# Row maxima that skip NaN: VectorE's write-backs end with tile 33, and the tiles behind it are divided anew into loads, passes and maxima

## The chip, the core and the metric

The kernel runs on one core of a Trainium2 chip. The metric is the time of one execution in microseconds (us) on the device; lower is better. The engines that matter are VectorE (DVE in the profile), ScalarE (ACT), GpSimd (POOL), and SyncE (SP), whose queue issues every load. TensorE does nothing here.

## The reference

```python
x = np.random.randn(32, 2048, 2048).astype(np.float32)
x[np.random.rand(32, 2048, 2048) < 0.1] = np.nan
def reference(x, axis):          # axis = -1
    return np.nanmax(x, axis=axis).astype(np.float32)
```

65536 rows of 2048 float32 numbers, a tenth of them NaN, are reduced to the largest number of each row that is not NaN. 537 MB are read and 0.26 MB written.

## The kernel before

The rows are spread over 128 partitions, so that each partition has 512 rows, 2048 quarters of a row (a quarter, Q, is 512 numbers). They are worked through in 69 tiles: tile 0 has 4 quarters, tiles 1 to 35 have 32, tiles 36 to 68 have 28. Three buffers `xt` take the tiles in turn, so tile n is loaded into the buffer of tile n-3.

A tile goes through four steps.

- SyncE issues its loads, one or several, as soon as the last maximum of tile n-3 is done (line 494).
- ScalarE makes passes (line 298, operation `Prelu`): from the upper 16 bits of each number it makes a key of 16 bits in which a NaN has become harmless. Up to tile 37 the key takes the place of the upper half in `xt`; from tile 38 on the keys stand in one of three key buffers (the names `kt` and, for the two that lie in the room between the buffers, `xt`).
- A write-back turns keys into upper halves again (times -1, plus a constant). GpSimd, ScalarE or VectorE can do it (lines 308, 298 and 315 `TENSOR_SCALAR`).
- VectorE takes the maxima (line 315 `TENSOR_REDUCE`), which need the write-backs of all their quarters.

At the end GpSimd and VectorE put NaN into rows that held nothing else (lines 330, 344, 322), and three stores write the result.

The order on every engine is the order in which the program records the work; nothing is moved afterwards, and semaphores hold an instruction back until what it reads is there. What is recorded is set by the table `TILES`, written out by hand, with one entry for each tile: the sizes of its loads; its passes, in groups, with the write-backs that follow each group; and the sizes of its maxima, all in quarters.

```python
    + [([32], [([12], [(5, -1), 7]), ([12], [12]), ([8], [8])], [12, 12, 8])] * 31
```

This is one load of 32 quarters, a pass of 12 followed by write-backs of 5 and 7, a pass of 12 with one of 12, a pass of 8 with one of 8, and maxima of 12, 12 and 8. A bare number is GpSimd's write-back. A pair names another engine:

```python
who = "pool" if wait is None else "act" if wait == 0 else "dve"
```

so `(5, -1)` is a write-back of 5 quarters by VectorE, `(7, 0)` one of 7 by ScalarE at once, and `(2, 1)` one of 2 by ScalarE after its next pass. The buffer's release and the load that waits for it are these lines:

```python
if state["red"] == len(reds):
    free[number % BUFS] = [state["end"]]
...
xt, before = room(number), free[number % BUFS]
```

Of the kernel before, what the change touches and what calls it, by code (L numbers as in the profile page):

```python
# [15 lines left out]

TILES = (
    [([4], [([4], [4])], [4])]
    + [([32], [([12], [(5, -1), 7]), ([12], [12]), ([8], [8])], [12, 12, 8])] * 31
# [8 lines left out]
    + [([28], [([7], [7]), ([9], [9]), ([12], [12])], [16, 12])] * 2  # L28
# [27 lines left out]
)  # L56


# [582 lines left out]
```

## Time and profile before

| | us |
|---|---|
| median of 3 runs (lowest to highest) | 1266.52 (1262.43 to 1266.83) |
| the profiled execution's own time | 1266.14 |
| its span, first to last instruction | 1264.0 |
| VectorE busy | 1194.2 |
| ScalarE busy | 1125.6 |
| GpSimd busy | 1073.0 |

The span is what the profile's times count in; the execution takes about 2 us more around it. In the views, `a <- b: us, times, longest` is idle time of a that ended when b was done; a row of the order of time has its start, its length, the engine, the line, the operation, what it writes and reads, and in brackets the idle time before it.

### The profile page before, as it was taken

How to read it: one execution, taken by the hardware profiler on the slowest of the kernel's cores; microseconds unless marked ns; L12 is line 12 of the kernel's file. 1: busy time of each engine (PE TensorE's matmuls, PEld its weight loads, DVE VectorE, ACT ScalarE, POOL GpSimd, SP SyncE). 2: the span in 40 equal slices, each digit the busy share in tenths (PEclk: the TensorE clock that was granted, in tenths of full speed). 3: DMA queues.
4: the chain of work that ended last, by engine and by line, in shares of the span. 5: the costliest groups of instructions: out<-in, count | busy, mean ns of one | idle time of the engine just before them, and what ended most of it. 6: DMA issues, size and time to landing. Idle time of an engine off the chain costs nothing.

```text
span 1264.0 us, 1010 instructions
## 1 busy us (share of the span) xinstructions
DVE 1194.2 (94%) x251; ACT 1125.6 (89%) x275; POOL 1073.0 (85%) x248
## 2 busy tenths in 40 slices
DVE  0899999999999999999999999998989989999999
ACT  3999999999999999999999877689777788989998
POOL 0888788888888888888899897867999989999998
DMA  9999999999999999999999999899999999999997
GB/s 413 442 440 431 431 431 431 431 432 431 431 431 438 444 440 433 436 431 431 422 436 433 376 385 436 377 436 436 434 430 414 436 436 426 435 428 433 429 428 307
DMA packets 16807, 537.20 MB, mean 425 GB/s; under 512 B 2592, under 2 KB 2592, under 8 KB 5152
## 3 DMA queue, kind: packets, MB, share of 16 engines
q1 hardware_dynamic: 16800, 537.14, 98.9%
q14 instruction: 7, 0.06, 0.0%
HBM read 536.87 MB, written 0.26 MB: 425 GB/s over the span
## 4 chain that ended last, share of the span: by engine, by line
DVE 38%; DMA 30%; ACT 17%; POOL 14%; issue 1%; SPq 0%; DVEq 0%; ACTq 0%
DVE acc L315 36%; DMA xt<-in_x_dram 30%; ACT xt L298 16%; POOL xt L308 14%; DVE xt L315 2%; ACT kt L298 1%; POOL late L330 0%; POOL acc L344 0%; SPq L285 0%; DVE acc L322 0%; DVEq L182 0%; SPq L636 0%; ACTq L182 0%; SPq L292 0%
## 5 line engine op out<-in xcount | busy, mean ns | idle before, releaser
L315 DVE TENSOR_REDUCE acc<-xt 128x3 f32<-128x6144 f32 (+3 forms) x210 | 1113.4, 5349 | 48.6 <-POOL xt L308 44.4
L308 POOL TENSOR_SCALAR xt<-xt 128x3584 int16<-128x3584 uint16 (+11 forms) x198 | 922.1, 4657 | 180.2 <-ACT xt L298 171.8
L298 ACT ACTIVATE xt<-xt 128x6144 uint16<-128x6144 int16 (+10 forms) x214 | 948.2, 4526 | 117.8 <-DMA xt<-in_x_dram 117.1
L298 ACT ACTIVATE kt<-xt 128x6144 uint16<-128x6144 int16 (+11 forms) x43 | 142.0, 3322 | 13.9 <-POOL xt L308 11.8
L308 POOL TENSOR_SCALAR xt<-kt 128x2048 int16<-128x2048 uint16 (+9 forms) x35 | 143.7, 4107 | 4.8 <-ACT kt L298 2.8
L315 DVE TENSOR_SCALAR xt<-xt 128x2560 int16<-128x2560 uint16 (+3 forms) x38 | 75.9, 1997 | 19.0 <-ACT xt L298 19.0
L298 ACT ACTIVATE xt<-kt 128x1536 int16<-128x1536 uint16 (+4 forms) x16 | 36.9, 2309 | 0.4
L315 DVE TENSOR_SCALAR xt<-kt 128x4096 int16<-128x4096 uint16 x2 | 8.0, 4020 | 0.0
L330 POOL TENSOR_SCALAR late<-acc 128x112 int32<-128x112 f32 (+1 forms) x5 | 4.9, 971 | 0.4
L298 ACT ACT_TABLE_LOAD x1 | 1.3, 1283 | 1.4 <-SPq L292 1.4
L344 POOL TENSOR_TENSOR acc<-acc,late 128x112 int32<-128x112 int32 (+1 forms) x5 | 2.0, 400 | 0.4
L350 POOL MEMSET scalars<- 128x1 f32 x1 | 0.1, 99 | 1.0 <-SPq L292 1.0
L622 POOL MEMSET const-float32-0.0<- 128x1 f32 x1 | 0.1, 99 | 0.2 <-issue 0.2
L298 ACT ACTIVATE scalars<-scalars 128x1 f32<-128x1 f32 x1 | 0.2, 203 | 0.0
L322 DVE SCALAR_TENSOR_TENSOR acc<-acc 128x7 f32<-128x7 f32 x1 | 0.2, 166 | 0.0
L622 POOL MEMSET const-bfloat16-1.0<- 128x1 bf16 x1 | 0.1, 103 | 0.0
L622 POOL MEMSET const-uint8-127<- 128x1 uint8 x1 | 0.1, 103 | 0.0
L622 POOL MEMSET const-float32-1.0<- 128x1 f32 x1 | 0.1, 99 | 0.0
## 6 DMA issues: line engine op xcount, KB each, us to landing
xt<-in_x_dram SPq DMA_DIRECT2D x21, 7168.0 KB, 22.4
xt<-in_x_dram SPq DMA_DIRECT2D x2, 4864.0 KB, 18.4
xt<-in_x_dram SPq DMA_DIRECT2D x4, 2304.0 KB, 26.8
xt<-in_x_dram SPq DMA_DIRECT2D x2, 4352.0 KB, 22.3
xt<-in_x_dram SPq DMA_DIRECT2D x2, 3584.0 KB, 25.4
xt<-in_x_dram SPq DMA_DIRECT2D x5, 1280.0 KB, 27.8
xt<-in_x_dram SPq DMA_DIRECT2D x2, 3072.0 KB, 20.6
xt<-in_x_dram SPq DMA_DIRECT2D x3, 2048.0 KB, 25.2
```

The costliest lines, as they stand in the source:

```text
L298: lambda: nc.scalar.activation(**kw),
L308: lambda: nc.gpsimd.tensor_scalar(**kw),
L315: return order.add("dve", nc.vector, lambda: do(**kw), deps)
L322: lambda: engine.scalar_tensor_tensor(out=acc, in0=acc, scalar=0.0, in1=acc, op0=ALU.mult, op1=ALU.add),
L330: lambda: engine.tensor_scalar(out=none, in0=acc, scalar1=LEAST, scalar2=float(0x00400000), op0=ALU.is_lt, op1=ALU.mult,),
L344: lambda: engine.tensor_tensor(out=bits, in0=bits, in1=none, op=ALU.add),
L350: e_top = order.add("pool", nc.gpsimd, lambda: nc.gpsimd.memset(top, EDGE), [])
L622: nc = _bacc.Bacc("TRN2", target_bir_lowering=False, num_devices=1)
```

## The change

Only the table `TILES` changes. Tile 32 becomes like tiles 1 to 31. Tile 33 keeps a write-back of 5 quarters by VectorE, and that is the last one; tiles 34, 35, 36, 37, 39, 42 and 46 had one each, of 2, 2, 4, 5, 4, 8 and 8 quarters. Tiles 33 to 68 get other loads, passes, write-backs and maxima; their sizes in total (32 and 28 quarters) and their buffers stay. There are 110 loads instead of 111 and 211 maxima instead of 210.

```diff
-    + [([32], [([12], [(5, -1), 7]), ([12], [12]), ([8], [8])], [12, 12, 8])] * 31
-    + [([23, 9], [([18, 6], [(6, -1), 6, 12]), ([8], [8])], [12, 12, 8])]
-    + [([19, 13], [([12], [(5, -1), 7]), ([10], [10]), ([10], [3, 7])], [12, 12, 8])]
-    + [([12, 20], [([12], [(2, -1), 10]), ([12], [12]), ([8], [8])], [12, 12, 8])]
-    + [([15, 17], [([12, 8, 6, 6], [(2, -1), 10, 5, 7, 8])], [12, 12, 8])]
-    + [([28], [([9], [5, (4, -1)]), ([7], [7]), ([7], [7]), ([5], [5])], [4, 12, 12])]
-    + [([28], [([10], [(5, -1), 5]), ([6], [6]), ([9], [9]), ([3], [3])], [16, 12])]
...
+    + [([32], [([12], [(5, -1), 7]), ([12], [12]), ([8], [8])], [12, 12, 8])] * 32
+    + [([18, 14], [([12], [(5, -1), 7]), ([6], [6]), ([6], [6]), ([8], [8])], [12, 12, 8])]
+    + [([12, 20], [([7, 8, 9, 8], [7, 8, 9, 8])], [12, 12, 8])]
+    + [([25, 7], [([6], [6]), ([6], [6]), ([7], [7]), ([5], [(2, 1), 3]), ([8], [8])], [12, 12, 8])]
+    + [([28], [([7], [7]), ([8], [8]), ([9], [9]), ([4], [4])], [4, 8, 3, 1, 4, 8])]
+    + [([28], [([11, 11], [10, 7, 5]), ([6], [6])], [8, 8, 4, 8])]
...
```

What stands in VectorE's row from tile 33 to the first maxima of tile 36 before (`TENSOR_SCALAR` is a write-back, `128x2560` its 5 quarters; `TENSOR_REDUCE` is a maximum, `128x3` its 3 rows):

```order
L315 TENSOR_SCALAR xt<-xt 128x2560
L315 TENSOR_REDUCE acc<-xt 128x3 x2
L315 TENSOR_REDUCE acc<-xt 128x2
L315 TENSOR_SCALAR xt<-xt 128x1024
L315 TENSOR_REDUCE acc<-xt 128x3 x2
L315 TENSOR_REDUCE acc<-xt 128x2
L315 TENSOR_SCALAR xt<-xt 128x1024
L315 TENSOR_REDUCE acc<-xt 128x3 x2
L315 TENSOR_REDUCE acc<-xt 128x2
L315 TENSOR_SCALAR xt<-xt 128x2048
L315 TENSOR_REDUCE acc<-xt 128x1
```

And the same place now (all lines behind the table have numbers smaller by 4):

```order
L311 TENSOR_SCALAR xt<-xt 128x2560
L311 TENSOR_REDUCE acc<-xt 128x3 x2
L311 TENSOR_REDUCE acc<-xt 128x2
L311 TENSOR_REDUCE acc<-xt 128x3 x2
L311 TENSOR_REDUCE acc<-xt 128x2
L311 TENSOR_REDUCE acc<-xt 128x3 x2
L311 TENSOR_REDUCE acc<-xt 128x2
L311 TENSOR_REDUCE acc<-xt 128x1
L311 TENSOR_REDUCE acc<-xt 128x2
L311 TENSOR_REDUCE xt<-xt 128x1
```

The write-backs ahead of the maxima of tiles 34, 35 and 36 are gone; the maxima of 34 and 35 are cut as before, those of 36 into six, one of which leaves its result in `xt` for the next.

GpSimd's row from tile 33 to tile 35 before, each row a write-back:

```order
L308 TENSOR_SCALAR xt<-xt 128x3584
L308 TENSOR_SCALAR xt<-xt 128x5120
L308 TENSOR_SCALAR xt<-xt 128x1536
L308 TENSOR_SCALAR xt<-xt 128x3584
L308 TENSOR_SCALAR xt<-xt 128x5120
L308 TENSOR_SCALAR xt<-xt 128x6144
L308 TENSOR_SCALAR xt<-xt 128x4096
L308 TENSOR_SCALAR xt<-xt 128x5120
L308 TENSOR_SCALAR xt<-xt 128x2560
L308 TENSOR_SCALAR xt<-xt 128x3584
L308 TENSOR_SCALAR xt<-xt 128x4096
```

And now:

```order
L304 TENSOR_SCALAR xt<-xt 128x3584
L304 TENSOR_SCALAR xt<-xt 128x3072 x2
L304 TENSOR_SCALAR xt<-xt 128x4096
L304 TENSOR_SCALAR xt<-xt 128x3584
L304 TENSOR_SCALAR xt<-xt 128x4096
L304 TENSOR_SCALAR xt<-xt 128x4608
L304 TENSOR_SCALAR xt<-xt 128x4096
L304 TENSOR_SCALAR xt<-xt 128x3072 x2
L304 TENSOR_SCALAR xt<-xt 128x3584
L304 TENSOR_SCALAR xt<-xt 128x1536
L304 TENSOR_SCALAR xt<-xt 128x4096
```

Tile 33 (27 quarters for GpSimd in both; rows 1 to 4 before, 1 to 3 now) has its middle write-backs of 10, 3 and 7 quarters cut into 6, 6 and 8; tile 34 (rows 5 to 7 before, 4 to 7 now) goes from 30 quarters in three to all 32 in four; tile 35 has 30 in both, in five instead of four, and its other two quarters go to ScalarE.

More of the change, by code (lines that the diff above doesn't have):

```diff
@@ L18 @@
     [([4], [([4], [4])], [4])]
-    + [([32], [([12], [(5, -1), 7]), ([12], [12]), ([8], [8])], [12, 12, 8])] * 31
[8 rows of a table removed]
-    + [([28], [([7], [7]), ([9], [9]), ([12], [12])], [16, 12])] * 2
[1 row of a table removed]
+    + [([32], [([12], [(5, -1), 7]), ([12], [12]), ([8], [8])], [12, 12, 8])] * 32
[10 rows of a table added]
     + [([28], [([9], [9]), ([12], [12]), ([7], [(7, 0)])], [8, 20])]
     + [([28], [([9], [9]), ([12], [3, 9]), ([7], [(7, 0)])], [12, 16])]
[24 rows of a table removed]
[2 rows of a table added]
+    + [([28], [([7], [7]), ([9], [9]), ([12], [12])], [16, 12])] * 3
+    + [([28], [([8], [1, (2, 2), 5]), ([6, 3], [9]), ([11], [11])], [16, 12])]
+    + [([28], [([6], [6]), ([10], [10]), ([12], [12])], [16, 12])]
+    + [([28], [([8], [8]), ([9], [9]), ([11], [11])], [8, 8, 12])] * 2
[6 rows of a table added]
+    + [([16, 12], [([8], [8]), ([8], [8]), ([12], [7, (5, 0)])], [8, 8, 12])] * 2
[7 rows of a table added]
 )
```

47 rows, old and new, of the table TILES are left out of this document.

## The prediction

> **What bounds the kernel now.** I read the page first, then the stages, then the chain of waits, then the order of time around the place where the stages differ.
>
> ```profile
> span 1264.0 us, 1010 instructions
> DVE 1194.2 (94%) x251; ACT 1125.6 (89%) x275; POOL 1073.0 (85%) x248
> q1 hardware_dynamic: 16800, 537.14, 98.9%
> ```
>
> The loads fill the DMA engines for nearly the whole span; VectorE is the fullest of the three engines. Which of the two sets the end can differ by stage, so the table of stages comes next (busy time of VectorE, ScalarE and GpSimd, then clock, DMA share and GB/s).
>
> ```profile
> 24.90:682.60 657.70, 633.15 (x134) 634.17 (x103) 552.88 (x107) 1.00 1.00 433
> 682.60:831.60 149.00, 147.55 (x26) 110.45 (x28) 127.89 (x27) 1.00 0.95 400
> 831.60:1205.10 373.50, 354.55 (x67) 323.59 (x96) 338.07 (x80) 1.00 1.00 430
> ```
>
> In one stage of 149 us the transfers fall to 400 GB/s, and there VectorE is 99% busy (147.55 of 149.00) while ScalarE has 39 us to spare. The chain of waits says the same (start, length, what):
>
> ```profile
> 56.95 26.05 DMA xt<-in_x_dram
> ...
> 83.03 13.93 ACT xt L298 x2
> ...
> 97.03 7.10 POOL xt L308
> ...
> 104.15 10.89 DVE acc L315 x2
> ...
> 579.38 25.74 DMA xt<-in_x_dram
> ...
> 657.13 5.60 DVE xt L315
> ...
> 807.91 23.66 DMA xt<-in_x_dram
> ...
> 1028.90 23.49 DMA xt<-in_x_dram
> ...
> 1083.16 29.16 DVE acc L315 x6
> 1112.32 1.07 issue
> 1113.39 73.70 DVE acc L315 x18
> 1187.10 74.45 DVE acc L315 x30
> ```
>
> A load's piece ends where the load lands. The rows from 83.03 on are one round of the steady loop: two passes of ScalarE, a write of GpSimd (its last, of 8 quarters, is still to come) and two maxima, done 32.0 us after the landing. Tile 4 lands at 56.95 + 26.05 = 83.00 and tile 31 at 605.12, so a tile of 32 quarters takes 522.12 / 27 = 19.34 us. Tile 43 lands at 831.57 and tile 56 at 1052.39, so one of 28 quarters takes 220.82 / 13 = 16.99 us. Between tile 31 and tile 43 stand four tiles of 32 and eight of 28: 4 x 19.34 + 8 x 16.99 = 213.3 us, but they took 831.57 - 605.12 = 226.45. **The loads lost 13.2 us there**, while the stages around run at 433 and 430 GB/s. From 657 to 808 the chain stands in VectorE and meets no load.
>
> Why VectorE held the loads up: the load of tile n goes into the buffer of tile n-3 and is issued when that tile's last maximum is done.
>
> ```profile
> SPq L494 <- DVE acc L315: 1165.8, 65, 43.6
> ...
> 618.00 1.67 DVE L315 TENSOR_SCALAR xt<-xt 128x2560 int16<-128x2560 uint16 x1
> ...
> 657.04 5.67 DVE L315 TENSOR_SCALAR xt<-xt 128x2560 int16<-128x2560 uint16 x1
> 662.82 17.34 DVE L315 TENSOR_REDUCE acc<-xt 128x3 f32<-128x6144 f32 x3
> 680.07 2.33 DVE L315 TENSOR_SCALAR xt<-xt 128x1024 int16<-128x1024 uint16 x1
> 682.50 17.34 DVE L315 TENSOR_REDUCE acc<-xt 128x3 f32<-128x6144 f32 x3
> 699.76 1.15 DVE L315 TENSOR_SCALAR xt<-xt 128x1024 int16<-128x1024 uint16 x1
> ...
> 718.27 3.13 DVE L315 TENSOR_SCALAR xt<-xt 128x2048 int16<-128x2048 uint16 x1
> ...
> 736.40 4.53 DVE L315 TENSOR_SCALAR xt<-xt 128x2560 int16<-128x2560 uint16 x1
> ...
> 770.62 5.87 POOL L308 TENSOR_SCALAR xt<-kt 128x5120 int16<-128x5120 uint16 x1
> 771.22 6.43 DVE L315 TENSOR_SCALAR xt<-xt 128x2048 int16<-128x2048 uint16 x1
> ```
>
> SyncE's queue waits for nothing but VectorE's maxima. From 657 on VectorE is never idle for long, and in between stand its own write-backs: 5.67 + 2.33 + 1.15 + 3.13 + 4.53 + 6.43 = 23.2 us to tile 39. The same write of 2560 numbers took 1.67 us at 618. The last two rows say what the rest is: GpSimd's write ends at 776.49, VectorE's, begun in the middle of it, at 777.65, 1.16 us later. It stood behind GpSimd's whole instruction.
>
> How late may a buffer be? Two more rows, of SyncE's queue (its first issue is tile 36's) and of ScalarE's waits for the landings of tiles 36 and 37:
>
> ```profile
> 680.19 38.52 SPq L494 DMA_DIRECT2D xt<-in_x_dram  x3
> 702.40 16.25 ACT L298 ACTIVATE xt<-xt 128x4608 uint16<-128x4608 int16 x4 [5.43 <-DMA xt<-in_x_dram]
> 719.37 16.39 ACT L298 ACTIVATE xt<-xt 128x5120 uint16<-128x5120 int16 x4 [0.72 <-DMA xt<-in_x_dram]
> ```
>
> Tile 36 was issued at 680.2 and landed at 702.4: 22.2 us, 5.2 more than its 16.99. Tile 37 was issued at 699.8, where tile 34's maxima ended, and landed at 719.4: 2.6 more. So a load that is to cost nothing is issued 2.6 to 5.2 us before the load ahead of it lands; call that lead. In the steady loop the lead is 25.74 - 19.34 = 6.4 us, after tile 43 it is 23.49 - 16.99 = 6.5; both cost nothing. I take 4.6 as needed, nearer the late end since that row shows a loss.
>
> **The change, part by part.** VectorE loses seven writes, two of them behind tile 39. Tile 32 becomes like the 31 before it, and tile 33 keeps one VectorE write. GpSimd and ScalarE take over the 33 quarters of tiles 34 to 46 that VectorE wrote. What GpSimd pays for them comes from these groups (busy and mean ns of one), and the last three rows are its work on a tile of 28 that it writes alone:
>
> ```profile
> L308 POOL TENSOR_SCALAR xt<-xt 128x4096 int16<-128x4096 uint16 x45 | 214.6, 4768 | 7.4 <-ACT xt L298 4.2
> L308 POOL TENSOR_SCALAR xt<-xt 128x3584 int16<-128x3584 uint16 x48 | 203.5, 4240 | 41.5 <-ACT xt L298 40.5
> L308 POOL TENSOR_SCALAR xt<-kt 128x2048 int16<-128x2048 uint16 x7 | 17.4, 2480 | 0.6 <-ACT kt L298 0.2
> ...
> 919.94 9.60 POOL L308 TENSOR_SCALAR xt<-xt 128x3584 int16<-128x3584 uint16 x2 [0.51 <-ACT xt L298]
> 929.62 7.04 POOL L308 TENSOR_SCALAR xt<-kt 128x6144 int16<-128x6144 uint16 x1
> 936.83 4.20 POOL L308 TENSOR_SCALAR xt<-xt 128x3584 int16<-128x3584 uint16 x1 [0.16 <-ACT xt L298]
> ```
>
> A quarter costs (4.77 - 2.48) / 4 = 0.573 us and an instruction 0.19, with 0.08 between two. GpSimd needs 16.9 us (919.94 to 936.83) for a tile that takes 16.99 to load: it keeps up, just. ScalarE's 39 us of spare time hold its new writes.
>
> Now the chain of tiles 33 to 36, whose maxima free the buffers of tiles 36 to 39. VectorE: 17.34 us of maxima for 32 quarters, as in the rows above, some 16.0 for tile 36, which is cut into six. Tile 32 lands at 605.12 + 19.34 = 624.5. By the round above GpSimd ends it 104.13 + 0.08 + 4.77 - 83.00 = 26.0 later, at 650.5, and VectorE 32.0 later; now it is free at 657.0, so I take 656.8 and 650.8.
>
> - Tile 33: its write (5 quarters) meets GpSimd's write of quarters 12 to 18, 655.1 to 658.7, ends 1.5 us behind it, at 660.2, and pushes GpSimd back by as much; with 6 and 8 quarters more GpSimd ends the tile at 668.6 (ScalarE is ahead). Maxima end at 677.6 (now 680.2). Lead of tile 36: its predecessor lands at 605.12 + 4 x 19.34 = 682.5, so 4.8 us (now 2.3).
> - Tile 34: GpSimd writes all 32 quarters, 4.20 + 4.77 + 5.34 + 4.77 and the gaps, 19.4 us, to 688.0. The first maximum waits 0.1 us for it; maxima end at 695.1 (now 699.8). Tile 36 lands at 699.5; lead 4.3.
> - Tile 35: 30 quarters in five writes, 18.5 us, to 706.5; maxima end at 712.8 (now 718.3). Tile 37 lands at 716.5; lead 3.7.
> - Tile 36: 28 quarters, 17.1 us, to 723.6; maxima end at 728.9 (now 736.4). Tile 38 lands at 733.5; lead 4.5.
>
> Of tiles 37 to 42 GpSimd writes 28, 24, 24, 21, 28 and 20 quarters, so it gains on the loads from tile 38 on, VectorE needs 15.2 of every 16.99 us, and the leads grow past 5. With 4.6 needed the losses are 0.3 (tile 37), about 0.65 (tile 38) and less behind, together **1.0 us**; with 2.6 needed they are 0, with 5.2 needed every lead from 36 on is a little short and they come to some 4. So the loads get back 13.2 - 1.0 = 12.2 us.
>
> Is it passed on to the end? VectorE runs from 1083.16 to 1261.58 with a gap of 1.07, so the end is set by when that run starts: 30.8 us after tile 56 lands. In the new tables tile 56 is cut into the same passes and maxima (9, 10, 9; 8, 8, 12), tile 57 loads whole, in passes 8, 8, 12, and the maxima behind are as long, two or three instructions fewer at some 0.1 us each. I cost the new tail at nothing; its cover is that GpSimd and ScalarE stay ahead of VectorE there, and where a split is worse by a us, the end is later by that.
>
> The sum: 1264.0 - 13.2 + 1.0 = 1251.8 us of span. The profiled execution took 1266.14, 2.1 over its span; that makes 1253.9, and the median of the runs, 1266.52, lies 0.4 above that execution: 1254.3, say 1254.
>
> The price of the one write left, in tile 33, is where a rule can be weighed. In rows: 1.67 us (at 618) if GpSimd happens to be idle, 3.3 by the meeting above, 5.67 as now. SBUF — State Buffer, section "Who interferes with whom", of the Trainium skill states an exclusive lock: of a VectorE instruction in a two-port mode and a GpSimd one, whoever starts first keeps the pair of ports and the other blocks fully. By that the price would be the rest of GpSimd's instruction plus the write, and the sum stays 1254; by the bare mean of the earlier tiles it would be 1253.8. The 6.43 us row that ends 1.16 us behind GpSimd's agrees with the rule.
>
> **The rivals.**
> ```profile
> POOL xt L308 <- ACT xt L298: 171.8, 94, 21.3
> ...
> 637.72 8.50 POOL xt L308
> ```
>
> 1. The stage is only half cured. GpSimd's work on tiles 34 to 37 is 19.4 + 18.5 + 17.1 + 17.1 = 72.1 us against 72.7 of loads, with nothing to spare, and ScalarE's passes come in other sizes; if GpSimd waits 1 to 2 us a tile for ScalarE, leads fall to 2 to 3 us until tile 40 and 1 to 2.5 us a tile are lost again, 4 to 9 in all: 1258 to 1262. For it: the first row, 94 such waits in this kernel. Against it: ScalarE makes 24 quarters in 13.93 us (at 83.03), 0.58 each, GpSimd needs 19.4 / 32 = 0.61 on tile 34, so from there on it does not catch up with the passes.
> 2. Nothing comes of it: the loads were slow in that stage for a cause of their own, and VectorE merely had the time. Then 1264 to 1268. Against it: the leads fall exactly there, and the loads are back at 430 GB/s as soon as the lead is.
> 3. Slower: GpSimd becomes the bound. Beside a VectorE write its 12 quarters took 8.50 us (the second row), 1.2 times 7.04. If its writes ran so for another reason, the four tiles above would cost 14 us more, and the eight or so later tiles that it writes alone (41, 45, 47 to 49, 51 to 53) would take 20 instead of 16.9, 25 us: about 1290. Writes 6% longer, 4 + 8 x 0.9, eat most of the gain; from about 10% on, 7 + 8 x 1.5 = 19, the kernel is slower. Against it: with VectorE's writes gone nothing is left in the trace that stretches GpSimd's, and the row at 929.62 has 7.04 beside maxima. Trainium Architecture — The Big Picture, "The five engines, in one table", of the Trainium skill counts streaming elementwise work among what GpSimd is not for, at half VectorE's speed, and so speaks against the move; by it the 33 quarters would cost 19 us of GpSimd instead of about 11 of VectorE. Here 0.573 us against 1.67 / 5 = 0.33 bears the ratio out, but VectorE's price with its waits was 23.2 us for 22 quarters to tile 39.
>
> **How the numbers follow.** The likeliest, 1254, with its own range 1251 to 1257 (losses of 0 to 4 us, and runs that differ by 4): 0.66. Half cured, 1257 to 1262: 0.18. Nothing, 1262 to 1268: 0.09. Slower: 0.07. The range 1251 to 1260 takes in the first and most of the second. About 0.5%, 6.3 us, is what a measurement tells from no change: faster is below 1260.2, 0.66 and three quarters of 0.18, 0.80; same is the rest of it with the third case and the milder part of the last, 0.15; slower 0.05.
>
> **What would show it.** Right: 430 GB/s between 682 and 832 on the same table of stages, tile 43 landing near 819.5, GpSimd and no longer VectorE without idle time from 660 to 745, no write by VectorE after 661, the last run of maxima starting near 1071. Wrong: landings of tiles 36 to 43 more than 17.5 us apart, or gaps in VectorE's run after 1075 that wait for GpSimd.

## The result, and the profile after

The changed kernel takes 1259.38 us (median of 6 runs, 1258.51 to 1260.26) against 1266.61 (1262.43 to 1266.89): a ratio of 0.9948, 95% interval 0.9935 to 0.9961. It is 7.2 us faster; 12.5 were forecast. The profiled execution took 1259.93 us. In a later lot the two ran beside each other again: 1259.01 (1258.73 to 1261.63) against 1263.79 (1259.22 to 1268.20), a ratio of 0.9964 (0.995 to 0.9979), 4.8 us. It is mainly the kernel before that varies.

The page's first lines and the busiest queue, after:

```profile
span 1258.1 us, 1009 instructions
DVE 1167.0 (93%) x245; ACT 1142.9 (91%) x287; POOL 1071.4 (85%) x249
q1 hardware_dynamic: 16656, 537.14, 99.1%
```

The table of stages, cut where tiles 35, 43 and 56 land now (columns as in the prediction):

```profile
24.90:682.50 657.60, 632.35 (x133) 632.69 (x105) 555.23 (x107) 1.00 1.00 434
682.50:820.40 137.90, 126.20 (x26) 124.89 (x36) 126.73 (x29) 1.00 0.99 426
820.40:1042.80 222.40, 197.20 (x30) 178.49 (x48) 192.67 (x39) 1.00 0.99 429
```

The stage of tiles 36 to 43 went from 149.0 to 137.9 us, from 400 to 426 GB/s, and VectorE has 11.7 us of idle time in it. But the stage behind, 222.4 us for 13 tiles, is 1.6 us longer than the 220.8 of before, and the end has its own loss. The chain of waits, after, at the three places:

```profile
729.19 22.60 DMA xt<-in_x_dram
...
784.13 19.33 DMA xt<-in_x_dram
...
1062.48 193.21 DVE acc L311 x54
```

The first two are the loads of tiles 39 and 42, whose buffers the chain waits for. The last is VectorE's closing run, 193.21 us without a pause, to the end. From the issues, landings and last maxima of each tile in the traces (lead as in the prediction; loss is the time between two landings less 16.91 us, which is what a tile of 28 quarters takes where the lead is long):

| tile | lead and loss before | lead and loss after | last maximum after landing: before, after |
|---|---|---|---|
| 36 | 2.4, 2.9 | 4.3, 0.0 | 34.1, 29.7 |
| 37 | 2.5, 0.1 | 4.0, 0.0 | 36.8, 28.9 |
| 38 | 1.0, 1.8 | 3.3, 1.7 | 33.3, 28.6 |
| 39 | 1.5, 2.7 | 5.7, 0.0 | 35.1, 32.3 |
| 40 | 1.5, 3.0 | 6.5, 0.0 | 30.3, 31.7 |
| 42 | 1.8, 3.0 | 1.4, 1.0 | 29.2, 28.0 |
| 52 | 5.5, 0.0 | 5.7, 0.5 | 27.4, 30.5 |
| 53 | 6.5, 0.0 | 3.1, 0.0 | 27.2, 30.4 |
| 54 | 6.3, 0.0 | 1.7, 1.9 | 28.1, 28.7 |
| 56 | 6.6, 0.0 | 5.3, 0.0 | 26.4, 30.5 |

The last load lands 9.4 us sooner (1247.5, was 1256.9), and the last maximum ends 8.15 us behind it, where it was 4.65. 9.4 - 3.5 = 5.9 is the gain of the span. So two things need a cause: leads that fall again at tiles 42, 53 and 54, and a closing run that starts late. (Tile 52 lost 0.5 with a lead of 5.7 that cost nothing in later runs.)

Both begin at a ScalarE pass. The order of time after, around tiles 39, 50 and 55, the last pass of each and GpSimd's write-back behind it, for tile 39 also the two ahead of it:

```profile
757.74 7.30 POOL L304 TENSOR_SCALAR xt<-xt 128x4096 int16<-128x4096 uint16 x2 [0.83 <-ACT xt L294]
...
765.07 5.32 ACT L294 ACTIVATE kt<-xt 128x6144 uint16<-128x6144 int16 x1 [3.65 <-POOL xt L304]
...
770.47 7.04 POOL L304 TENSOR_SCALAR xt<-kt 128x6144 int16<-128x6144 uint16 x1 [5.44 <-ACT kt L294]
...
952.12 4.90 ACT L294 ACTIVATE kt<-xt 128x5632 uint16<-128x5632 int16 x1 [4.19 <-POOL xt L304]
...
957.10 6.48 POOL L304 TENSOR_SCALAR xt<-kt 128x5632 int16<-128x5632 uint16 x1 [5.01 <-ACT kt L294]
...
1038.71 5.32 ACT L294 ACTIVATE kt<-xt 128x6144 uint16<-128x6144 int16 x1 [4.97 <-POOL xt L304]
...
1044.12 4.20 POOL L304 TENSOR_SCALAR xt<-kt 128x3584 int16<-128x3584 uint16 x1 [5.44 <-ACT kt L294]
```

Each time ScalarE idles until GpSimd has finished a write-back (in tile 39 at 765.04), only then makes the pass, and GpSimd then idles for the length of that pass. GpSimd loses 5 us at each place, and the maxima from there on end late: tile 39's 32.3 us after its landing and tile 51's 32.5, where the first kernel below has 28.5 and 28.3.

Why does ScalarE wait? From tile 38 on a pass needs a free key buffer, and in the tiles of a list `EARLY` the last pass waits for the next buffer as well:

```python
kold = freed(key, (key + 1) % NKEYS) if number in EARLY and at + c == end else freed(key)
```

And where one maximum needs one write-back of ScalarE and one of GpSimd, `joints` lets the two count on one common semaphore, so that VectorE waits once. The code knows ScalarE's write-back then only by that common count, unless a later ScalarE instruction has been recorded. In these three tiles a short write-back of ScalarE, 4, 2 and 1 quarters (`(4, 2)`, `(2, 2)`, `(1, 1)`), stands right ahead of the last pass, and its partner is a write-back of GpSimd that is still running. The next buffer, which ScalarE itself has already read out, counts as taken until GpSimd is done. The order of ScalarE's row shows it, with the semaphores named, and what a kernel without the early wait has instead (-, +):

```text
 L294 ACTIVATE xt<-xt 128x2048 [waits order_act]
-L294 ACTIVATE kt<-xt 128x6144 [waits order_pair39_2]
+L294 ACTIVATE kt<-xt 128x6144 [waits order_pool]
```

That reading is theory A below; it rests on the code and was then tried.

### The profile page after: what moved, and what is told of

It is laid out like the page before. It is cut to its first block, busy times and chain, and to the rows that moved or that the text cites. A ratio compares the mean times of both kernels' runs of the same rounds, so it can differ in the third digit from the quotient of the medians.

```text
span 1258.1 us, 1009 instructions
## 1 busy us (share of the span) xinstructions
DVE 1167.0 (93%) x245; ACT 1142.9 (91%) x287; POOL 1071.4 (85%) x249
## 4 chain that ended last, share of the span: by engine, by line
DMA 33%; DVE 28%; POOL 20%; ACT 19%; issue 1%; SPq 0%; DVEq 0%
DMA xt<-in_x_dram 33%; DVE acc L311 28%; POOL xt L304 20%; ACT xt L294 17%; ACT kt L294 2%; DVE xt L311 0%; SPq L281 0%; SPq L490 0%; DVE acc L318 0%; SPq L632 0%; DVEq L178 0%; SPq L288 0%
## 5 line engine op out<-in xcount | busy, mean ns | idle before, releaser
L311 DVE TENSOR_REDUCE acc<-xt 128x3 f32<-128x6144 f32 (+4 forms) x210 | 1112.3, 5347 | 69.8 <-POOL xt L304 64.4
L304 POOL TENSOR_SCALAR xt<-xt 128x4096 int16<-128x4096 uint16 (+9 forms) x201 | 921.0, 4582 | 156.2 <-ACT xt L294 145.4
L294 ACT ACTIVATE xt<-xt 128x6144 uint16<-128x6144 int16 (+14 forms) x224 | 960.7, 4382 | 74.0 <-DMA xt<-in_x_dram 73.5
L294 ACT ACTIVATE kt<-xt 128x6144 uint16<-128x6144 int16 (+10 forms) x41 | 140.9, 3452 | 31.1 <-POOL xt L304 30.9
L304 POOL TENSOR_SCALAR xt<-kt 128x6144 int16<-128x6144 uint16 (+10 forms) x33 | 145.3, 4403 | 21.2 <-ACT kt L294 19.2
L311 DVE TENSOR_SCALAR xt<-xt 128x2560 int16<-128x2560 uint16 x33 | 55.5, 1683 | 19.0 <-ACT xt L294 19.0
L294 ACT ACTIVATE xt<-kt 128x1536 int16<-128x1536 uint16 (+6 forms) x20 | 43.9, 2201 | 0.4
```

Source lines behind the costliest of these rows:

```text
L294: lambda: nc.scalar.activation(**kw),
L304: lambda: nc.gpsimd.tensor_scalar(**kw),
L311: return order.add("dve", nc.vector, lambda: do(**kw), deps)
```

## The experiments

The kernels ran in three lots, each lot beside the kernel before on one chip; there it took 1262.12, 1263.79 and 1262.01 us, less than the 1266.6 from which the first expectations count. Theory A: the common semaphore frees a key buffer late. Theory B: GpSimd has too much to write from tile 39 on. C to J stand in the expectations.

### Without the early wait

```diff
-EARLY = (0, 1, ..., 38, 39, 40, ..., 49, 50, 51, ..., 54, 55, 56, 63)
+EARLY = (0, 1, ..., 38, 40, ..., 49, 51, ..., 54, 56, 63)
```

> The changed kernel, but in tiles 39, 50 and 55 ScalarE's last pass no longer waits for the key buffer after its own as well; the next tile's second pass waits for that one instead. Work, sizes and every write-back's engine are the same. Theory A (late keys): in these three tiles that second buffer is given free by a semaphore which ScalarE's short write-back shares with a later write-back of GpSimd, so the pass starts 3.7 to 5 us late and GpSimd then idles 5.4, 5.0 and 5.4 us. Without it the loads get back the 1.0 us of tile 42 and the 0.4 and 1.9 us of tiles 52 and 54, and VectorE's last run starts 3.6 us sooner after tile 56: 6.9 us in all, about 1252.5 us. Theory B (GpSimd is too full from tile 39 on): its work is unchanged, so 1258 to 1260 us.

(The buffer in question is that of the next tile's first pass, not of its second.)

Measured: 1252.12 us (1251.97 to 1252.73), ratio to before 0.992 (0.990 to 0.9939). The pass of tile 39 and GpSimd's writes around it, in this kernel:

```profile
757.15 7.31 POOL L304 TENSOR_SCALAR xt<-xt 128x4096 int16<-128x4096 uint16 x2 [0.83 <-ACT xt L294]
...
760.69 5.30 ACT L294 ACTIVATE kt<-xt 128x6144 uint16<-128x6144 int16 x1
...
766.07 7.05 POOL L304 TENSOR_SCALAR xt<-kt 128x6144 int16<-128x6144 uint16 x1 [1.61 <-ACT kt L294]
```

The pass starts beside GpSimd's writes instead of behind them, and GpSimd waits 1.61 instead of 5.44 us. The stages of tiles 36 to 43 and 44 to 56:

```profile
682.50:819.40 136.90, 125.83 (x27) 125.51 (x37) 125.77 (x29) 1.00 1.00 435
819.40:1039.40 220.00, 197.57 (x29) 182.28 (x49) 196.83 (x40) 1.00 1.00 434
```

The leads of tiles 42, 52 and 54 are 5.2, 5.7 and 5.5 us with no loss, and tile 56's maxima end 26.4 us after its landing, as in the kernel before. GpSimd's work is the same to the instruction, so theory B is out.

### Semaphores of their own

```diff
-pairs[number] = joints(keys, backs, reds)
+pairs[number] = {} if number in (39, 50, 55) else joints(keys, backs, reds)
```

> The changed kernel, but in tiles 39, 50 and 55 ScalarE's and GpSimd's write-backs each count on their own engine's semaphore instead of one that they share; ScalarE's last pass still waits for the next key buffer, and VectorE waits for two semaphores at four maxima. Theory A: the buffer is then free as soon as ScalarE's own write-back is done, and the time is that of the kernel without the early wait, about 1252.5 us, within 1 us. Theory B: 1258 to 1260 us. A third possibility, C, that the early wait itself and not the shared semaphore is what costs: it stays at 1258 to 1260 us while the kernel without the early wait gains.

Measured: 1252.20 us (1251.90 to 1253.13), ratio 0.9922 (0.990 to 0.9944). The early wait is still there and costs nothing, so C is out: it is the common semaphore. Waits of ScalarE for GpSimd's key buffers and of GpSimd for those passes, after and here:

```profile
ACT kt L294 <- POOL xt L304: 30.9, 16, 5.0
POOL xt L304 <- ACT kt L294: 19.2, 8, 5.4
```

```profile
POOL xt L304 <- ACT kt L294: 10.5, 9, 3.4
ACT kt L294 <- POOL xt L304: 7.8, 12, 1.7
```

The longest of ScalarE's waits goes from 5.0 to 1.7 us, and 23 of 31 us of them are gone.

### One half of the change alone

The tables of tiles 43 to 68 of before behind the new tiles 32 to 42, and the reverse.

> Tiles 0 to 42 as in the changed kernel, tiles 43 to 68 as before. Theory A: the loads still lose 1.6 us at tile 38 and 1.0 us at tile 42, but nothing at tiles 52 and 54, and VectorE's last run starts 30.8 us after tile 56 lands, as before; that is 13.4 - 2.6 = 10.8 us below the kernel before, about 1256 us. Theory B: the same or up to 2 us more, since GpSimd writes fewer quarters in tiles 43 to 46. Theory D (the last run of VectorE can't start sooner than it did, whatever the loads do): 1259 us or more.

> Tiles 0 to 42 as before, VectorE's write-backs of tiles 33 to 42 among them; tiles 43 to 68 as in the changed kernel. Theory A: the loads lose the 13.4 us of before, and 0.4 and 1.9 us more at tiles 52 and 54, and VectorE's last run starts 3.6 us later: 1266.6 + 5.9, about 1272 us, slower than before. Theory D: 1266 us, since the last run would start where it did.

Measured: new front and old back 1253.78 us (1253.65 to 1254.41), ratio 0.9934 (0.9912 to 0.9956); old front and new back 1267.73 (1266.41 to 1273.54), ratio 1.0052 (1.0033 to 1.0072). The front half of the change is worth the gain, the back half, with the late passes of tiles 50 and 55, takes some of it back. Both times came out 2 to 4 us below the expected ones, but those count from 1266.6; against the kernel before in the same lot the first gained 8.3 us (10.8 expected) and the second lost 5.6 (5.4). In the first, tile 39 still costs 1.0 us at tile 42, but tile 38 lost 1.0 instead of 1.7. In the second the loads of tiles 36 to 42 lost 11 us instead of 13.7, most of them with leads of 2.4 down to -0.1; how much a load with such a lead loses varies from run to run. Theory D is out by the first kernel: its last maximum ends at 1249.4 us, where it was 1261.6.

### Only tile 55

```diff
-EARLY = (..., 54, 55, 56, 63)
+EARLY = (..., 54, 56, 63)
```

> The changed kernel, but only tile 55's last pass no longer waits for the second key buffer; tiles 39 and 50 stay as they are. Theory A: only the start of VectorE's last run comes back, 3.6 us, and the loads lose as before: about 1255.7 us if the changed kernel runs at 1259.4. Theory H (the lateness of tiles 50 to 54 reaches the tail by itself): less than 1 us comes back.

> The changed kernel once more, on the same chip as the three others, to compare them with: 1258 to 1260 us by every theory.

Measured on one chip: 1255.41 (1255.04 to 1256.74) and the changed kernel 1259.01 (1258.73 to 1261.63). The difference is 3.6 us, as expected, and the last maximum ends 4.7 us behind the last landing instead of 8.2: tile 55 alone makes the closing run late. H is out. With 1252.1 above, from another chip, 3.3 of the 6.9 us fall to tiles 39 and 50.

### Who writes, with the cut left as it was

```diff
-([9], [5, (4, -1)])
+([9], [5, 4])         # to GpSimd, or [5, (4, 0)], to ScalarE; so in all seven tiles
```

> The kernel before, cut as it was; only the seven write-backs that VectorE made in tiles 34 to 46 go to GpSimd. Theory F (the writes on VectorE cost the loads, through GpSimd's lock): VectorE is rid of some 18 us to tile 39, GpSimd gets 17 quarters there at 0.573 us and five more instructions, and needs 19.4 + 19.7 + 17.4 + 17.4 = 73.9 us for tiles 34 to 37 against 72.7 of loads, so leads stay at 2 to 4 us and part of the 13.4 us stays lost, some 5 us: 1255 to 1261 where the kernel before has 1266. Theory G (the new division is what gains, not who writes): within 2 us of the kernel before.

> The kernel before, cut as it was; the seven write-backs of VectorE in tiles 34 to 46 go to ScalarE. Theory F: VectorE is rid of the same work, GpSimd has no more than before (70 us for tiles 34 to 37), ScalarE has room for 33 quarters at 0.573 us, 19 us, in the 39 us that it waited there; most of the 13.4 us come back: 1253 to 1258. Theory G: within 2 us of the kernel before.

Measured: to GpSimd 1261.38 (1258.50 to 1265.64), ratio 0.9969 (0.995 to 0.9989); to ScalarE 1264.32, ratio 0.9981 (0.9959 to 1.0003), in two groups, four runs at 1257.5 to 1258.2 and six at 1264.3 to 1264.9. Beside the kernel before at 1263.79 the first lies between the theories, 2.4 us lower and 0.4 above F's range. For ScalarE the median is where G has it, and F has missed; the four shorter runs are at the upper end of what F gives. The trace of the GpSimd kernel's profiled run, one of the long ones (1265.64), and that of the kernel before, at tile 32:

```profile
634.23 17.18 POOL L308 TENSOR_SCALAR xt<-xt 128x3072 int16<-128x3072 uint16 x3 [2.11 <-ACT xt L298]
638.09 8.73 DVE L315 TENSOR_SCALAR xt<-xt 128x3072 int16<-128x3072 uint16 x1
```

```profile
633.99 17.04 POOL L308 TENSOR_SCALAR xt<-xt 128x3072 int16<-128x3072 uint16 x3 [2.65 <-ACT xt L298]
637.36 2.01 DVE L315 TENSOR_SCALAR xt<-xt 128x3072 int16<-128x3072 uint16 x1
```

It is the same write of 6 quarters, 2.01 or 8.73 us. GpSimd's second write there starts at 637.96 in the one and 637.72 in the other; where VectorE's stands ready 0.36 us ahead of it, GpSimd is pushed back, and where it comes 0.13 us behind, VectorE waits 7 us.

### The same without tile 32's cut

```diff
-([23, 9], [([18, 6], [(6, -1), 6, 12]), ([8], [8])], [12, 12, 8])      # tile 32
+([32], [([12], [(5, -1), 7]), ([12], [12]), ([8], [8])], [12, 12, 8])
```

> The kernel before with its seven VectorE write-backs of tiles 34 to 46 given to ScalarE, and tile 32 cut like tiles 1 to 31. Theory J (a race at tile 32): in the cut of before, VectorE's write of tile 32 is ready at 637.3 to 638.1 us and GpSimd's write of 12 quarters starts between 637.7 and 638.0; where GpSimd is first, VectorE waits 7 us, and the run is about 6.5 us longer. Without that cut there is no run at 1264 to 1265, all are at 1255 to 1258.5. Against it (the two groups of times have another cause): times of both groups again.

Measured: 1258.66 (1257.62 to 1260.12), ratio 0.997 (0.9956 to 0.9985); one group, none of its 10 runs near 1264. J holds for the upper group, though seven runs lie up to 1.6 us above the range, and the race itself was seen only in the other kernel's long run. So taking VectorE's writes away without a new cut gains some 3 us in that lot, where the kernel before ran at 1262.0.

Why not more? In its trace the loads of tiles 36 to 40 still lose 6.6 us: 2.1 at tile 36, behind the write that VectorE keeps in tile 33 (6.32 us here), and 3.0 at tile 40, which waits for tile 37's maxima. Around those GpSimd waits for ScalarE, and VectorE for GpSimd:

```profile
713.35 11.58 POOL L307 TENSOR_SCALAR xt<-xt 128x3584 int16<-128x3584 uint16 x3 [3.48 <-ACT xt L297]
...
732.53 3.65 POOL L307 TENSOR_SCALAR xt<-xt 128x3072 int16<-128x3072 uint16 x1 [3.48 <-ACT xt L297]
736.21 8.69 DVE L314 TENSOR_REDUCE acc<-xt 128x4 f32<-128x8192 f32 x1 [4.69 <-POOL xt L307]
```

The same two waits of GpSimd were 0.98 and 0.41 us in the kernel before; ScalarE's two new writes there take 2.47 and 3.04. So with the old cut they make GpSimd late instead, and the new division is a part of the cure, not only who writes.

### VectorE's writes put back into the best kernel

```diff
-([7, 8, 9, 8], [7, 8, 9, 8])              # tile 34; likewise 35, 36 and 37
+([7, 8, 9, 8], [(2, -1), 5, 8, 9, 8])
```

> The kernel without the early wait in tiles 39, 50 and 55, with VectorE's write-backs of tiles 34 to 37 put back (2, 2, 4 and 5 quarters, taken from GpSimd's). Theory F (a write on VectorE costs more than it spares GpSimd, since it stands behind GpSimd's instruction): the four writes took 2.33, 1.15, 3.13 and 4.53 us in the kernel before; leads of tiles 37 to 40 fall from 4 to between 2 and below 0, and the loads lose 1 to 3 us at each of them: 1255 to 1260 us against 1252.1. Theory G (the division is what counts, not who writes): 1251.5 to 1253 us, since GpSimd gets 7.4 us less to do there.

Measured: 1261.63 (1260.99 to 1262.75), ratio to before 0.9997 (0.9981 to 1.0012), 9.5 us above the same kernel without them in the first lot, and 9.2 above the next section's kernel in this one. VectorE's writes in it, and GpSimd's that the first two meet:

```profile
676.81 5.29 POOL L304 TENSOR_SCALAR xt<-xt 128x4608 int16<-128x4608 uint16 x1
...
677.90 4.79 DVE L311 TENSOR_SCALAR xt<-xt 128x1024 int16<-128x1024 uint16 x1
...
699.85 4.73 POOL L304 TENSOR_SCALAR xt<-xt 128x4096 int16<-128x4096 uint16 x1
...
700.04 5.13 DVE L311 TENSOR_SCALAR xt<-xt 128x1024 int16<-128x1024 uint16 x1
...
722.53 1.29 DVE L311 TENSOR_SCALAR xt<-xt 128x2048 int16<-128x2048 uint16 x1
...
739.35 1.79 DVE L311 TENSOR_SCALAR xt<-xt 128x2560 int16<-128x2560 uint16 x1
```

The two short ones, of 2 quarters, take longest: they stand behind GpSimd's writes of 5.29 and 4.73 us that began at 676.81 and 699.85. It is also what SBUF — State Buffer, section "Who interferes with whom", of the Trainium skill says of the lock, here with 4.79 us for a write that took as little as 1.15. Tile 35's maxima end at 722.6 instead of 712.2. Leads of tiles 37 and 38 fall to -0.6 and -3.1, and they lose 3.1 and 5.5 us. G is out. F has the cause; the time lies 1.6 us above its range, since two tiles lost more than the 3 us that it gave each.

### Without VectorE's last write

```diff
-([18, 14], [([12], [(5, -1), 7]), ...      # tile 33
+([18, 14], [([12], [(3, 0), 9]), ...
```

> The kernel without the early wait in tiles 39, 50 and 55, and VectorE's last write-back, of 5 quarters in tile 33, goes to ScalarE (3) and GpSimd (2 more in its write of 7). VectorE spares the 3.4 us that the write took in the changed kernel, GpSimd gets 1.15 us more and is pushed back by 1.4 us less. Theory F: leads of tiles 36 to 38 stay at 4 or rise by up to 0.5, the loss of 0 to 1 us at tile 38 goes: 1251.2 to 1252.2 us. If GpSimd bounds tiles 34 to 36 instead of VectorE, nothing changes: 1252.1.

Measured: 1252.39 (1251.94 to 1253.22), no change from 1252.12. Tile 33's maxima end 30.7 us after the landing instead of about 34, but those of tiles 34 to 36 no sooner (31.7, 29.9, 29.1, where the kernel without the early wait has 31.3, 29.6, 28.7). VectorE waits 3.02 us for GpSimd ahead of tile 34's maxima: GpSimd bounds these tiles, and the write left in tile 33 cost nothing here. The prediction had it between nothing and 0.5 us (1253.8 or 1254.3).

## Why the prediction was right or wrong, point by point

- **What bounded the kernel** held: the 13 us lost at tiles 36 to 42 were the loads' wait for VectorE, whose writes stood behind GpSimd's, and putting four of them back into the new division costs 9.5 us. It is not the whole account: with the old cut, taking them away gained some 3.
- **The chain of tiles 33 to 36** held. Ends of maxima: forecast 677.6, 695.1, 712.8, 728.9; measured 678.2, 695.4, 713.0, 729.2. GpSimd's ends were 0.1 to 0.4 us off. The write of tile 33 took 3.4 us (3.3 by the meeting in the prediction):

```profile
657.38 3.37 DVE L311 TENSOR_SCALAR xt<-xt 128x2560 int16<-128x2560 uint16 x1
```

- **The loss that stays, 1.0 us**, failed, and with it the sentence that leads grow past 5 from tile 38 on: they did at tiles 39 to 41 and fell to 1.4 at tile 42. Tile 38 lost 1.7 instead of 0.65; that is a size (0 to 1.0 in six other runs with leads of 3.6 to 4.2, so no fixed lead of 4.6 decides it). Tiles 42, 44 and 54 lost 3.2 more, all of it gone without the early wait, and that was a missing term: the counts of quarters said that GpSimd keeps up, but not that it gets its keys in time. The order with the semaphores named, `order_pair39_2` on ScalarE's last pass, told it beforehand; I read the order for the work on each engine and not for what it waits for.
- **"I cost the new tail at nothing"** failed. Its cover, that GpSimd and ScalarE stay ahead of VectorE, was gone at tile 55 before the closing run began: 3.5 us in this trace, the same semaphore. I compared the cut of tiles 56 and 57 and not of 55, from which the run takes its start.
- The last load landed at 1247.5, 2.8 us later than the 1256.9 - 12.2 = 1244.7 that the sum implies. These 2.8 and the tail's 3.5 make the 6.3 by which the span, 1258.1, lies above the 1251.8 of the sum. With the semaphores apart the span is 1250.3, without the early wait 1251.0: the rest of the sum was right within 1.5 us.
- **The gain** was forecast from an execution of 1266.14, in the upper part of the kernel before's 1258.6 to 1268.2. Even the repaired kernel gained only 10.0 us beside the kernel before in its lot.
- **The signs.** One of those for wrong came true: tiles 38 and 42 landed 18.6 and 17.9 us after the tile ahead. VectorE wrote nothing after 661, and from 682.6 to 831.6 the loads ran at 425 GB/s instead of 430.
- **The rivals.** The first, half cured, named the right size (1258 to 1262), by luck, and the wrong place: GpSimd did wait for ScalarE, but at tiles 39, 50 and 55, not through 34 to 37. The second and third are out: the loads came back to 426 to 435 GB/s, and GpSimd's 12 quarters took 7.04 and 7.05 us.

## What to carry to other kernels

Where an engine has no time to spare, adding up its work is not enough: for every instruction that it is fed by, look in the order of the program at which semaphore that feeder waits for and who else counts on it. A semaphore that two engines share spares its reader a wait, but everything freed by it is freed as late as the later of the two. And a short write-back that can meet a long one of another engine, as VectorE's met GpSimd's here (1.15 or 5.13 us for 2 quarters), should be priced with the wait, or moved.

## What the runs showed of the hardware that I had not expected

- Whether VectorE or GpSimd is first at a common moment decides 7 us. By 0.36 us one way the write took 2.01, by 0.13 us the other way 8.73. The kernel before spread over 9 us on the later chips (1258.6 to 1268.2) at a clock of 1.0 throughout; the three others with tile 32 cut as before spread over 7, all those with tile 32 cut like its predecessors over 0.8 to 2.9, also where VectorE's writes were put back. The race does not make all of it: in the kernel before's own long execution, 1266.14 us, VectorE was first. What else does was not shown.
- A load that comes late does not lose what it is late by. With a lead of 3.1 tile 43 lost nothing after the change, with 1.4 tile 42 lost 1.0, with 1.5 tiles 39 and 40 lost 2.7 and 3.0 in the kernel before. And losses of 1.0 and 0.5 us also came with leads of 5.5 (tile 40, semaphores of their own) and 12.9 us (tile 62, writes to ScalarE). Many losses lie near 1, 2 or 3 us, many others between; what sets them stays open.
